# Residual loads on ScalarE's queue, the last conv rows kept on chip, and a conv layer norm in smaller steps

## The chip, the cores and the metric

The kernel runs on one core of one Trainium2 chip. The metric is the device time of one execution in microseconds; the median of three runs is the time before.

## The reference

One layer of a streaming encoder for 512 prompt frames and 64 sample frames. Only the last part matters here: a conv branch with a layer norm over channels, and one output projection over three concatenated branches, added to the scaled input and normalised.

```python
def conv_branch(a, b, left, conv_w, conv_b, ln_g, ln_b, w_pw):
    ...
    y = layer_norm(y + conv_b, ln_g, ln_b)
    y = jax.nn.silu(y) @ w_pw
    return y, up[:, -(CONV_W - 1):]

def layer_step(...):
    ca, cb, cg, q, k, v, ag, mq, mg = split_in_proj(x @ w_in)
    ...
    mix = jnp.concatenate([conv_out * jax.nn.silu(cg), att * jax.nn.silu(ag), mem * jax.nn.silu(mg)], axis=-1)
    y = layer_norm(ALPHA * x + mix @ w_out, ln_g, ln_b)
```

All is fp32, 1024 conv channels, 512 attention and 512 memory channels, model width 2048.

## The kernel before

TensorE works on pairs of reduced-precision pieces of each fp32 number: a weight block `wraw` (128 x 1024) is cast to `whi` by ScalarE (L248), and VectorE takes the rest as `wlo` (L253); a product is `hi*hi + lo*hi + hi*lo`. A *stage* is one such weight block and the matmuls that use it. `next_stage` hands out the pieces of stage i, casts the blocks up to i + 2, and loads further ones as far ahead as `AHEAD` and, for the output projection, `AHEAD_OUT` (by the block's form) say. Weight loads go out on SyncE's queue (L175); the sums of two blocks that some forms need are made by accumulating loads on GpSimd's queue (L179), of a copy that ScalarE makes (L198).

The order of the stages is fixed: V, the input projection's column pairs, keys and queries, the memory parts; then `out_pair(8, ...)` twice (14 stages each, output columns 0 to 1023 and 1024 to 2047), which multiplies the attention and memory half of the mix by its half of the output weights and stores the results in DRAM as `a_dram`; then the pointwise projection of the conv branch (8 stages, `pw`); then `out_pair(0, ...)`, the conv half for columns 0 to 1023 (14 stages, numbered 0 to 13 below); then two plain blocks of four stages for columns 1024 to 1535 and 1536 to 2047, and the last layer norm. The 14 stages of `out_pair` are seven products of two stages each, in the order of `OUT_FORMS`. TensorE's queue has stages 10 and 11 of the second call, and part of the stages behind them, right behind stage 7.

Work beside the matmuls is written as generators (`sides`), and `pump` moves each on by one `yield` after a stage. `conv_ln` is the one in `sides["norm"]`: it loads the eight channel blocks `y` of the conv from DRAM on SyncE (L964), where the conv had spilled them (L532), subtracts the mean (L971), sums squares (ScalarE squares L976, VectorE adds `s`, L977), and has TensorE sum them over the partitions (`var`, L985). Then come `rs` on VectorE, a power on GpSimd (L990), a diagonal `dg` on VectorE, `ra` and `rb` on TensorE (L999, L1000), copies to `rstd` on ScalarE (L1002), a multiply and a Silu for each block (L1005, L1006). `split_sx` makes the hi and lo pieces `sx` (L1018, L1019) that the pointwise stages use.

`z[t, n]` is the residual and the result, one tile for each of five token tiles t and four column blocks n. `load_z` loads a piece of x on SyncE (L1165), multiplies it by ALPHA on ScalarE (L1166) and adds `a_dram` by an accumulating load on GpSimd (L1167). The z of columns 0 to 1023 are loaded from the pointwise stage 3 on, one or two a stage; the other ten partly inside `out_pair(0, ...)` and partly when it has been written out. The tile scheduler keeps for each engine the order in which it takes the instructions; each engine waits in that order.

Of the kernel before, what the change touches and what calls it, by code (L numbers as in the profile page):

```python
# [51 lines left out]
AHEAD_OUT = {"a11": 5, "s1": 6, "s2": 0, "a12": 4, "s3": 6, "s4": 6, "a22": 4}  # L52
# [76 lines left out]
def hymba_kernel(ctx: ExitStack, tc: tile.TileContext, wst, xT, memT, xp, xs, kcT, vc, mkcT, mvc, biasx,  # L129
# [368 lines left out]
    def queue_conv(j):  # L498
# [24 lines left out]
        def last():  # L523
            t = TAPS - 1
            y = t6([P, NT], "y")
            o = NP_TOK + 30
            for w, o, ys in ((HP, 0, slice(0, HP)), (HS, o, slice(HP, HALF))):
                yv = y.rearrange("p (a b) -> p a b", a=2)[:, :, ys]
                uv, av = (m.rearrange("p (a b) -> p a b", a=2)
                          for m in (up[0][:, o + t:o + t + 2 * w], acc[0][:, o:o + 2 * w]))  # L530
                nc.vector.scalar_tensor_tensor(yv, uv, cw_sb[:, j, t:t + 1], av, op0=ALU.mult, op1=ALU.add)
            spill.append(lambda: nc.gpsimd.dma_start(y_dram[j], y))  # L532
            if j == 0:
                s1[0] = y
            elif j == 1:
                y0, s1[0] = s1[0], t6([P, NT], "s1")
                nc.vector.tensor_add(s1[0], y0, y)
            else:
                nc.vector.tensor_add(s1[0], s1[0], y)
            if j == NCB - 1:  # L540
                sides["norm"].append(conv_ln())
# [417 lines left out]
    def conv_ln():  # L959
        yield  # L960
        spill.pop()()
        for j in range(NCB):
# [7 lines left out]
        for j in range(NCB):  # L970
# [7 lines left out]
            if j == 3:  # L978
# [25 lines left out]
        for j in range(NCB):  # L1004
            nc.vector.tensor_mul(ysb[j], ysb[j], rstd)  # L1005
            nc.scalar.activation(ysb[j], ysb[j], AF.Silu, bias=cp_sb[:, 2, j:j + 1], scale=cp_sb[:, 1, j:j + 1])  # L1006
            if j == 3:
                yield
        for j in range(SX_EARLY):
            split_sx(j)  # L1010
        ln_left[0] = False
# [146 lines left out]

    def load_z(n, tiles=range(5)):

        for t in tiles:
            rows = P if t < 4 else NS_TOK
            ns = slice(n * 512, (n + 1) * 512)
            zt = z[t, n] = t5([P, 512], "z")
            nc.sync.dma_start(zt[:rows], xp[t * P:(t + 1) * P, ns] if t < 4 else xs[:, ns])  # L1165
            nc.scalar.mul(zt[:rows], zt[:rows], ALPHA)  # L1166
            nc.gpsimd.dma_start(zt[:rows], a_dram[t, n][:rows], accum_op=ALU.add)  # L1167
# [79 lines left out]
    for j in range(NCB):  # L1247
# [10 lines left out]
        if j >= 3:  # L1258
            load_z((j - 3) // 3, ((0, 1), (2, 3), (4,))[(j - 3) % 3])
# [69 lines left out]

    def conv_forms(stage):  # L1330
        if stage < 4:
            form234(stage, alloc_large)

# [18 lines left out]
    def zsample(i, acc):  # L1352
        zsum(4, i, out_source(4, acc))
        done(4, i)
        if i == 0:
            load_z(2, range(2))

    sub = nc.vector.tensor_sub
    load_z(1, (4,))
# [3 lines left out]
    load_z(2, range(2, 5))  # L1363
    load_z(3)
    g = load_g(2)
    accs, sacc = tileB(mlhs2, range(4), msl, list(range(8)))
# [117 lines left out]
```

## Time and profile before

| | us |
|---|---|
| median of three runs | 962.25 |
| lowest and highest | 959.97 and 962.35 |
| the profiled execution | 963.6 |
| its span | 961.8 |
| TensorE's matmuls busy | 931.7 |
| VectorE, ScalarE, GpSimd busy | 740.1, 480.4, 145.3 |
| mean granted TensorE clock | 0.981 |

The profile is of one execution. In the rows below times are from the start of the span; L and a number is a line of the kernel; `PE`, `DVE`, `ACT`, `POOL` and `SP` are TensorE, VectorE, ScalarE, GpSimd and SyncE, and a q behind a name its queue of DMA issues. Granted clock 1.00 is 2.4 GHz and .50 is 1.2 GHz. What stands in brackets is how long the engine was idle before the instruction, and what ended that.

### The profile page before, as it was taken

What the parts mean: (1) busy time and instruction counts of PE and PEld (TensorE: products, weight loads), DVE (VectorE), ACT (ScalarE), POOL (GpSimd) and SP (SyncE); (2) the same over time, 40 slices, a digit from 0 to 9 for tenths busy, and PEclk for the clock granted to TensorE, in tenths of its full rate; (3) what the DMA queues carried; (4) which work ended last, traced back from release to release, by engine and by line L of the source; (5) the groups of instructions that cost most, each with busy time, mean ns of one, the idle gap of its engine ahead of it and who ended that gap; (6) DMA issues with size and microseconds to landing.
All of it is one profiled execution on the core that took longest, in us unless ns stands there. A gap on an engine that the chain in (4) does not pass through costs nothing. (4 is left out here: it accounts for less than half of the span.)

```text
span 961.8 us, 15450 instructions
## 1 busy us (share of the span) xinstructions
PE 931.7 (97%) x5965; PEld 855.8 (89%) x5965; DVE 740.1 (77%) x1075; ACT 480.4 (50%) x805; POOL 145.3 (15%) x215
## 2 busy tenths in 40 slices
PE   8999999999999999999999999999988999978995
PEld 5899999999999999999999888998866899955873
DVE  7968986996799797688999564299998766737566
ACT  6655444454544444554554466646768643742200
POOL 0020000100110000011110001100122211333451
PEclk9999999999999999999999999999999999987997
DMA  9755566555666766589766558863883976996304
GB/s 327 208 171 147 145 164 174 160 147 165 198 178 173 195 169 184 183 233 242 181 173 167 165 175 225 211 156 80 198 268 105 248 279 183 196 217 204 98 19 179
DMA packets 61996, 175.34 MB, mean 182 GB/s; under 512 B 7710, under 2 KB 12318, under 8 KB 61922
## 3 DMA queue, kind: packets, MB, share of 16 engines
q1 hardware_dynamic: 41602, 111.92, 34.9%
q0 software_dynamic: 16720, 54.91, 28.1%
q10 hardware_dynamic: 3600, 7.52, 2.2%
q8 instruction: 47, 0.77, 0.3%
q14 instruction: 27, 0.22, 0.1%
HBM read 150.69 MB, written 23.63 MB: 181 GB/s over the span
## 5 line engine op out<-in xcount | busy, mean ns | idle before, releaser
L248 ACT CAST whi<-wraw 128x1024 fp32r<-128x1024 f32 x195 | 203.3, 1050 | 188.6 <-PE st L556 51.4
L253 DVE TENSOR_TENSOR wlo<-wraw,whi 128x1024 fp32r<-128x1024 f32 x173 | 215.2, 1247 | 95.1 <-ACT whi L248 48.0
L556 PE MATMUL st<-x,whi 128*128 128x288 f32 x1024 | 204.6, 295 | 0.0
L519 DVE SCALAR_TENSOR_TENSOR acc<-up,cw_sb,acc 128x606 f32<-128x606 f32 x232 | 196.5, 847 | 4.1
L556 PEld LDWEIGHTS st<-x,whi 128*128 128x128 f32 x1024 | 164.1, 188 | 0.3 <-ACT neg L625 0.2
L556 PE MATMUL st<-x,wlo 128*128 128x288 f32 x512 | 151.1, 295 | 0.0
L315 PE MATMUL accA<-x,whi 128*128 128x288 f32 x768 | 134.9, 298 | 0.0
L315 PEld LDWEIGHTS accA<-x,whi 128*128 128x128 f32 x768 | 112.8, 189 | 1.6 <-issue 0.8
L556 PEld LDWEIGHTS st<-x,wlo 128*128 128x128 f32 x512 | 96.1, 188 | 0.0
L315 PE MATMUL accA<-x,wlo 128*128 128x288 f32 x384 | 82.3, 296 | 0.0
L556 PE MATMUL st<-t13h,wlo 128*128 128x288 f32 x256 | 75.6, 295 | 0.0
L556 PE MATMUL st<-t13l,whi 128*128 128x288 f32 x256 | 75.5, 295 | 0.0
L556 PE MATMUL st<-t13h,whi 128*128 128x288 f32 x256 | 75.5, 295 | 0.0
L1116 PE MATMUL ob<-whi,mix 128*128 128x512 f32 x176 | 58.6, 413 | 4.5 <-ACT whi L248 4.5
L315 PEld LDWEIGHTS accA<-x,wlo 128*128 128x128 f32 x384 | 61.8, 189 | 0.0
L179 POOL DMA_DIRECT2D wraw<-in_wst_dram x27 | 27.1, 1003 | 177.5 <-DVE pos L612 60.1
L556 PE MATMUL st<-t,whi 128*128 128x288 f32 x256 | 51.3, 295 | 0.0
L179 POOL DMA_DIRECT2D wsum<-in_wst_dram x22 | 21.4, 974 | 190.1 <-ACT wsum L209 115.9
L556 PEld LDWEIGHTS st<-t13h,whi 128*128 128x128 f32 x256 | 48.1, 188 | 0.0
L556 PEld LDWEIGHTS st<-t13l,whi 128*128 128x128 f32 x256 | 48.1, 188 | 0.0
L556 PEld LDWEIGHTS st<-t13h,wlo 128*128 128x128 f32 x256 | 48.1, 188 | 0.0
L235 DVE TENSOR_TENSOR wraw<-wraw,wraw 128x1024 f32<-128x1024 f32 x33 | 40.2, 1218 | 7.5 <-DMA wraw<-in_wst_dram 7.3
(390 smaller groups left out, 1859.6 us busy)
## 6 DMA issues: line engine op xcount, KB each, us to landing
wraw<-in_wst_dram SPq DMA_DIRECT2D x151, 512.0 KB, 4.3
wraw<-in_wst_dram POOLq DMA_DIRECT2D x27, 512.0 KB, 8.1
wsum<-in_wst_dram POOLq DMA_DIRECT2D x22, 512.0 KB, 7.7
wlo<-in_wst_dram POOLq DMA_DIRECT2D x22, 512.0 KB, 7.3
xraw<-in_xT_dram SPq DMA_DIRECT2D x19, 288.0 KB, 6.3
ad<-c POOLq DMA_DIRECT2D x16, 256.0 KB, 4.7
z<-in_xp_dram SPq DMA_DIRECT2D x16, 256.0 KB, 10.1
z<-ad POOLq DMA_DIRECT2D x16, 256.0 KB, 7.0
```

The costliest lines, as they stand in the source:

```text
L179: nc.gpsimd.dma_start(dst, wst[where[b]], accum_op=ALU.add)
L235: nc.vector.tensor_add(a21, a21, w_fetch(q[{"s1": "a22", "s2": "a11", "s4": "a12"}[form]]))
L248: nc.scalar.copy(hi, src)
L253: nc.vector.tensor_sub(lo, src, hi.bitcast(F32))
L315: nc.tensor.matmul(acc[:, :HALF], stat[:, ws], mv[:, c], start=ki == 0 and pi == 0, stop=ki == len(klist) - 1 and pi == 2)
L519: nc.vector.scalar_tensor_tensor(acc[0], up[0][:, t:t + ACCW], cw_sb[:, j, t:t + 1], acc[0], op0=ALU.mult, op1=ALU.add)
L556: nc.tensor.matmul(acc[:, :HALF], stat[:, ws], mv, start=first and k == 0 and i == 0, stop=k == 7 and i == 2, skip_group_check=not first)
L1116: nc.tensor.matmul(a, stat[:, os_], mv[:, ws], start=first and ki == 0 and i == 0, stop=ki == 3 and i == 2, skip_group_check=not first)
```

## The change

Four things are done.

- `AHEAD_OUT` rises by one for three forms, so their blocks are loaded a stage earlier.
- The last block of conv rows, `y` 7, is written into a `t5` buffer and stays there; it is neither spilled nor loaded.
- `conv_ln` begins five steps after it is queued, not one, loads seven blocks, and yields after every second block in the loops (subtraction, Silu, `sx`), where it yielded once in the first two and not in the third.
- `load_z` loads on ScalarE's queue and only notes the tile; `form_z` multiplies and accumulates later. Columns 0 to 1023 are loaded in the pointwise stages 0 to 5; the ten z of the others one a stage from stage 8 of `out_pair(0, ...)` as written, and two a stage in the block behind it.

```diff
@@ -49,7 +49,7 @@
 AHEAD_PAIRS = 7
 SX_EARLY = 5
 OUT_FORMS = ("a11", "s1", "s2", "a12", "s3", "s4", "a22")
-AHEAD_OUT = {"a11": 5, "s1": 6, "s2": 0, "a12": 4, "s3": 6, "s4": 6, "a22": 4}
+AHEAD_OUT = {"a11": 5, "s1": 6, "s2": 0, "a12": 5, "s3": 7, "s4": 6, "a22": 5}
 
 
 def quads(pair):
@@ -522,14 +522,17 @@
 
         def last():
             t = TAPS - 1
-            y = t6([P, NT], "y")
+            y = t6([P, NT], "y") if j < NCB - 1 else t5([P, NT], "y")
             o = NP_TOK + 30
             for w, o, ys in ((HP, 0, slice(0, HP)), (HS, o, slice(HP, HALF))):
                 yv = y.rearrange("p (a b) -> p a b", a=2)[:, :, ys]
                 uv, av = (m.rearrange("p (a b) -> p a b", a=2)
                           for m in (up[0][:, o + t:o + t + 2 * w], acc[0][:, o:o + 2 * w]))
                 nc.vector.scalar_tensor_tensor(yv, uv, cw_sb[:, j, t:t + 1], av, op0=ALU.mult, op1=ALU.add)
-            spill.append(lambda: nc.gpsimd.dma_start(y_dram[j], y))
+            if j < NCB - 1:
+                spill.append(lambda: nc.gpsimd.dma_start(y_dram[j], y))
+            else:
+                ysb[j] = y
             if j == 0:
                 s1[0] = y
             elif j == 1:
@@ -957,9 +960,9 @@
         return a, b
 
     def conv_ln():
-        yield
-        spill.pop()()
-        for j in range(NCB):
+        for _ in range(5):
+            yield
+        for j in range(NCB - 1):
             ysb[j] = t5([P, NT], "y")
             nc.sync.dma_start(ysb[j], y_dram[j])
         a, b = bcast_sum(s1[0], "mean")
@@ -975,7 +978,7 @@
                 sq = t6([P, NT], "sq")
                 nc.scalar.activation(sq, ysb[j], AF.Square)
                 nc.vector.tensor_add(s2, s2, sq)
-            if j == 3:
+            if j % 2:
                 yield
         yield
         yield
@@ -1004,10 +1007,12 @@
         for j in range(NCB):
             nc.vector.tensor_mul(ysb[j], ysb[j], rstd)
             nc.scalar.activation(ysb[j], ysb[j], AF.Silu, bias=cp_sb[:, 2, j:j + 1], scale=cp_sb[:, 1, j:j + 1])
-            if j == 3:
+            if j % 2:
                 yield
         for j in range(SX_EARLY):
             split_sx(j)
+            if j % 2:
+                yield
         ln_left[0] = False
 
     shi, slo = [], []
@@ -1156,15 +1161,24 @@
 
     z = {}
 
+    zload = deque()
+
     def load_z(n, tiles=range(5)):
 
         for t in tiles:
             rows = P if t < 4 else NS_TOK
             ns = slice(n * 512, (n + 1) * 512)
-            zt = z[t, n] = t5([P, 512], "z")
-            nc.sync.dma_start(zt[:rows], xp[t * P:(t + 1) * P, ns] if t < 4 else xs[:, ns])
-            nc.scalar.mul(zt[:rows], zt[:rows], ALPHA)
-            nc.gpsimd.dma_start(zt[:rows], a_dram[t, n][:rows], accum_op=ALU.add)
+            z[t, n] = t5([P, 512], "z")
+            nc.scalar.dma_start(z[t, n][:rows], xp[t * P:(t + 1) * P, ns] if t < 4 else xs[:, ns])
+            zload.append((t, n))
+
+    def form_z(count):
+
+        for _ in range(min(count, len(zload))):
+            t, n = zload.popleft()
+            zt = z[t, n][:P if t < 4 else NS_TOK]
+            nc.scalar.mul(zt, zt, ALPHA)
+            nc.gpsimd.dma_start(zt, a_dram[t, n][:P if t < 4 else NS_TOK], accum_op=ALU.add)
 
     a_dram = {(t, n): dram([P, 512], "ad") for t in range(5) for n in range(4)}
 
@@ -1255,8 +1269,9 @@
         split_mix(j)
         if j in (1, 2, 3, 4):
             form1(j - 1, True)
-        if j >= 3:
-            load_z((j - 3) // 3, ((0, 1), (2, 3), (4,))[(j - 3) % 3])
+        form_z(2)
+        if j < 6:
+            load_z(j // 3, ((0, 1), (2, 3), (4,))[j % 3])
     drain()
 
 
@@ -1327,9 +1342,19 @@
         return spool.tile([P, 4, P] if i == 3 else [P, 2, HP], F32R, tag="t5" if i == 2 else "t9",
                           bufs=N5 if i == 2 else KD, name=nm(name))
 
+    ztiles = [(t, n) for n in (2, 3) for t in range(5)]
+
+    def next_z(count):
+        form_z(count)
+        for _ in range(min(count, len(ztiles))):
+            t, n = ztiles.pop(0)
+            load_z(n, (t,))
+
     def conv_forms(stage):
         if stage < 4:
             form234(stage, alloc_large)
+        elif stage >= 8:
+            next_z(1)
 
     def zsum(t, n, acc, op=None):
         zt = z[t, n][:P if t < 4 else NS_TOK]
@@ -1352,18 +1377,16 @@
     def zsample(i, acc):
         zsum(4, i, out_source(4, acc))
         done(4, i)
-        if i == 0:
-            load_z(2, range(2))
 
     sub = nc.vector.tensor_sub
-    load_z(1, (4,))
+    form_z(2)
     out_pair(0, {"p1": zsink(0, 0, False), "p5": zsink(1, 1, False, sub), "p16": zsink(1, 0, False),
                  "p2": zsink(0, 0, True), "p167": zsink(1, 1, True, sub), "p53": zsink(1, 0, True),
                  "p1674": zsink(0, 1, True, sub), "sample": zsample}, conv_forms)
-    load_z(2, range(2, 5))
-    load_z(3)
     g = load_g(2)
-    accs, sacc = tileB(mlhs2, range(4), msl, list(range(8)))
+    accs, sacc = tileB(mlhs2, range(4), msl, list(range(8)), before=lambda s: next_z(2))
+    while zload:
+        next_z(2)
     gs = (g, load_g(3))
     for t in range(4):
         settle(t, 2, accs[t], g, False)
```

What this does to the engines' order is shown at three places. Lines of the changed kernel are some numbers further down: the z load is its L1172, the multiply L1180, the accumulate L1181.

ScalarE, in `out_pair(0, ...)`, before: `z` with L1166 is the multiply, `whi` the casts of stages 7 to 11, `ztmp` the copy of a sample result.

```order
L1166 ACTIVATE z_9177<-z_9177 128x512
L1166 ACTIVATE z_9181<-z_9181 128x512
L248 CAST whi_9104<-wraw_9064 128x1024
L1166 ACTIVATE z_9327<-z_9327 128x512
L248 CAST whi_9125<-wsum_9027 128x1024
L1166 ACTIVATE z_9331<-z_9331 128x512
L1166 ACTIVATE z_9335<-z_9335 64x512
L248 CAST whi_9145<-wsum_9066 128x1024
L1166 ACTIVATE z_9339<-z_9339 128x512
L248 CAST whi_9185<-wraw_8751 128x1024
L1166 ACTIVATE z_9343<-z_9343 128x512
L248 CAST whi_9203<-wraw_8823 128x1024
```

And in the changed kernel, where `whi_9062` is the cast of stage 5 and `whi_9122` that of stage 8:

```order
L1172 DMA z_9176<-in_xp_dram 128x512
L198 COPY wsum_9029<-wraw_8764 128x1024
L248 CAST whi_9062<-wraw_8832 128x1024
L1180 ACTIVATE z_9176<-z_9176 128x512
L1172 DMA z_9198<-in_xp_dram 128x512
L248 CAST whi_9084<-wraw_8983 128x1024
L1172 DMA z_9226<-in_xp_dram 128x512
L1180 ACTIVATE z_9198<-z_9198 128x512
L1172 DMA z_9248<-in_xp_dram 128x512
L248 CAST whi_9101<-wraw_9027 128x1024
L1180 ACTIVATE z_9226<-z_9226 128x512
L248 CAST whi_9122<-wsum_8985 128x1024
```

The loads of z stand on ScalarE's own queue among the casts, each multiply one to four rows behind its load. It goes on in that way: the multiply of `z_9248`, the cast of stage 9, two loads, the cast of stage 10, a multiply, a load, two multiplies, the cast of stage 11.

SyncE, same place, before: the weights of stages 6 (`wraw_9025`) and 7 (`wraw_9064`), with seven z loads around them, and then those of stages 12 and on.

```order
L175 DMA wraw_9025<-in_wst_dram 128x1024
L1165 DMA z_9177<-in_xp_dram 128x512
L1165 DMA z_9181<-in_xp_dram 128x512
L175 DMA wraw_9064<-in_wst_dram 128x1024
L1165 DMA z_9327<-in_xp_dram 128x512
L1165 DMA z_9331<-in_xp_dram 128x512
L1165 DMA z_9335<-in_xs_dram 64x512
L1165 DMA z_9339<-in_xp_dram 128x512
L1165 DMA z_9343<-in_xp_dram 128x512
L175 DMA wraw_9189<-in_wst_dram 128x1024
L175 DMA wraw_9207<-in_wst_dram 128x1024
L175 DMA wraw_9209<-in_wst_dram 128x1024
```

In the changed kernel, where `wraw_8983` and `wraw_9027` are the weights of stages 6 and 7 and `wraw_9146` those of stage 12:

```order
L175 DMA wraw_8766<-in_wst_dram 128x1024
L1284 DMA gbraw_8918<-in_lngb_dram 5x512
L175 DMA wraw_8832<-in_wst_dram 128x1024
L175 DMA wraw_8983<-in_wst_dram 128x1024
L175 DMA wraw_9027<-in_wst_dram 128x1024
L175 DMA wraw_9146<-in_wst_dram 128x1024
L175 DMA wraw_9182<-in_wst_dram 128x1024
L175 DMA wraw_9204<-in_wst_dram 128x1024
```

No z load stands between the weights any more.

TensorE, at the seam of the two `out_pair(8, ...)`, before: `var` is the sum of squares, `ob` and `os` with `t_1094` and `xd` the end of the first pair, `mix_7302` the start of the second.

```order
L1116 MATMUL ob_1024_7332<-wlo_7833,t_1094_7628 128x512
L1120 MATMUL os_1061_7482<-whi_7832,xd_7432 128x512
L1122 MATMUL os_1061_7482<-wlo_7833,xd_7432 128x512
L985 MATMUL var_7911<-ones,s_1130_7817 128x1 x4
L985 MATMUL var_7911<-ones,s_1130_7817 64x1
L1116 MATMUL ob_1151_7938<-whi_7871,mix_7302 128x512 x2
L1116 MATMUL ob_1152_7939<-whi_7871,mix_7302 128x512 x2
L1120 MATMUL os_1153_7940<-whi_7871,mixsamp_7305 128x512
```

In the changed kernel, in the second pair, from the end of stage 7 (`mixsamp_7424`, `wlo_8040`) into stage 8 (`whi_8061`):

```order
L988 MATMUL var_8081<-ones,s_1144_7910 128x1 x4
L988 MATMUL var_8081<-ones,s_1144_7910 64x1
L1127 MATMUL os_1131_7868<-wlo_8040,mixsamp_7424 128x512
L1121 MATMUL ob_1129_7866<-whi_8061,t23h_7428 128x512
L1121 MATMUL ob_1129_7866<-whi_8061,t23l_7429 128x512
L1121 MATMUL ob_1129_7866<-wlo_8062,t23h_7428 128x512
L1121 MATMUL ob_1130_7867<-whi_8061,t23h_7428 128x512
L1121 MATMUL ob_1130_7867<-whi_8061,t23l_7429 128x512
L1121 MATMUL ob_1130_7867<-wlo_8062,t23h_7428 128x512
L1121 MATMUL ob_1129_7866<-whi_8061,t23h_7494 128x512
L1121 MATMUL ob_1129_7866<-whi_8061,t23l_7495 128x512
L1121 MATMUL ob_1129_7866<-wlo_8062,t23h_7494 128x512
```

`var` has moved from the seam to the end of the second pair's stage 7; `ra`, which stood in that pair's stage 1, is the next row behind these, after nine matmuls of stage 8.

## Rows read from the trace of the kernel before

**Rows 1.** page, busy us (share of the span) and instructions of each engine.

```profile
PE 931.7 (97%) x5965; PEld 855.8 (89%) x5965; DVE 740.1 (77%) x1075; ACT 480.4 (50%) x805; POOL 145.3 (15%) x215
```

**Rows 2.** windows: stretch, its length, busy us of each engine, PE clock, DMA share, GB/s.

```profile
777.00:797.00 20.00, 20.00 (x152) 20.00 (x151) 12.42 (x20) 9.19 (x15) 1.62 (x3) 1.00 0.63 214
695.00:750.00 55.00, 49.57 (x207) 39.01 (x206) 46.64 (x67) 36.93 (x52) 14.16 (x18) 0.94 0.63 188
850.00:895.00 45.00, 35.52 (x118) 25.33 (x117) 30.77 (x34) 18.00 (x22) 19.92 (x16) 0.81 0.78 207
```

**Rows 3.** windows of 5 us in the first of the two stretches.

```profile
725.00:730.00 5.00, 5.00 (x22) 4.08 (x20) 3.42 (x8) 1.07 (x3) 3.70 (x3) 0.72 0.20 74
745.00:750.00 5.00, 5.00 (x16) 3.92 (x16) 3.50 (x3) 3.64 (x5) 3.14 (x4) 0.67 0.80 139
```

**Rows 4.** waits of PE, 690 to 750: us in total, times, longest.

```profile
PE var L985 <- DVE s L977: 2.6, 1, 2.6
PE ob L1116 <- ACT whi L248: 1.7, 1, 1.7
```

**Rows 5.** timeline of ACT, 684 to 746: start, us, instruction, count, idle before.

```profile
731.99 6.19 ACT L1006 ACTIVATE y<-y,cp_sb 128x576 f32<-128x576 f32 x8
738.09 2.96 ACT L1018 CAST sx<-y 128x576 fp32r<-128x576 f32 x5
```

**Rows 6.** timeline of PE, 846 to 894.

```profile
845.65 0.39 PE L1116 MATMUL ob<-whi,t23h 128*128 128x512 f32 x1
...
850.19 0.39 PE L1122 MATMUL os<-wlo,mixsamp 128*128 128x512 f32 x1
854.92 1.22 PE L1116 MATMUL ob<-whi,mix 128*128 128x512 f32 x2 [4.34 <-ACT whi L248]
...
876.67 0.63 PE L343 MATMUL accB<-whi,mix 128*128 128x512 f32 x1
...
893.81 0.40 PE L343 MATMUL accB<-whi,mix 128*128 128x512 f32 x1
```

**Rows 7.** timeline of ACT, 836 to 878.

```profile
843.91 0.63 ACT L1166 ACTIVATE z<-z 128x512 f32<-128x512 f32 x1 [1.92 <-DVE z L1336]
849.96 0.63 ACT L1166 ACTIVATE z<-z 128x512 f32<-128x512 f32 x1 [5.42 <-DMA z<-in_xp_dram]
853.82 1.04 ACT L248 CAST whi<-wraw 128x1024 fp32r<-128x1024 f32 x1 [3.23 <-DMA wraw<-in_wst_dram]
...
869.84 1.04 ACT L248 CAST whi<-wraw 128x1024 fp32r<-128x1024 f32 x1 [5.92 <-DMA wraw<-in_wst_dram]
```

**Rows 8.** timeline of SP's queue, 780 to 895.

```profile
809.09 1.26 SPq L1165 DMA_DIRECT2D z<-in_xp_dram  x2
...
838.80 1.71 SPq L1165 DMA_DIRECT2D z<-in_xp_dram  x2
840.62 0.38 SPq L175 DMA_DIRECT2D wraw<-in_wst_dram  x1
...
863.26 5.76 SPq L175 DMA_DIRECT2D wraw<-in_wst_dram  x5
877.63 0.33 SPq L1165 DMA_DIRECT2D z<-in_xp_dram  x1
```

**Rows 9.** timeline of all engines, 724 to 729.5.

```profile
725.02 2.59 POOL L990 TENSOR_TENSOR rs<-rs,mhalf 128x8 f32<-128x8 f32 x1 [1.63 <-DVE rs L989]
...
728.84 0.83 PE L999 MATMUL ra<-dg,ones 128*128 128x128 f32 x6
```

**Rows 10.** DMA issues of ACT's queue: count, KB each, median us to landing.

```profile
gated<-neg ACTq DMA_DIRECT2D x8, 288.0 KB, 4.4
```

**Rows 11.** timeline of ACT, 800 to 882.

```profile
817.35 0.63 ACT L1166 ACTIVATE z<-z 128x512 f32<-128x512 f32 x1 [4.79 <-DMA z<-in_xp_dram]
...
880.68 0.63 ACT L1166 ACTIVATE z<-z 128x512 f32<-128x512 f32 x1 [3.19 <-DMA z<-in_xp_dram]
```

**Rows 12.** page, DMA issues: count, KB each, median us to landing.

```profile
z<-in_xp_dram SPq DMA_DIRECT2D x16, 256.0 KB, 10.1
```

## The prediction

> **What bounds the kernel now.** I read the busy shares first: TensorE's matmuls fill 97% of the span [rows 1], so only TensorE's own losses matter, and there are two kinds, idle time and a slow clock. The windows show where they are. A good stretch, 777 to 797, has PE busy for all of its 20 us at granted clock 1.00; two stretches have not [rows 2].
>
> *Stretch A*, 695 to 750, the conv layer norm: busy 49.57 of 55, so 5.4 us idle [rows 2]. Two of its 5-us windows ran slow: 5.00 us at .72 and 5.00 at .67 [rows 3], so 1.40 + 1.65 = 3.1 us lost. **A costs 8.5 us.** The reader is to see the causes on PE's waits: 2.6 us until DVE's sum of squares is there for `var`, 1.7 us until ScalarE casts a weight [rows 4]. That cast was late because eight Silu (6.19 us) and five `sx` casts (2.96 us) stood ahead of it on ScalarE in one block [rows 5].
>
> *Stretch B*, 850 to 895, the first half of the last output projection: busy 35.52 of 45, so 9.5 us idle, at mean clock .81 [rows 2], another 0.19 x 35.5 = 6.7 us. **B costs 16.2 us.** Its longest wait, 4.34 us, names ScalarE's weight cast as what ended it [rows 6], so the question goes to ScalarE's queue: it waited 5.42 us for a z load, 3.23 and 5.92 us for weight loads [rows 7]. SyncE's queue says why the weights were late: z loads went out between them from 838.80, and the next weight could not go out until 863.26 [rows 8].
>
> **The change part by part.** *Last conv rows on chip.* One store and one load fewer, both off TensorE's path: nothing by itself.
>
> *Layer norm in smaller steps.* `var` and its inputs move from the seam between the two output pairs to the end of the second pair's stage 7, and all weight casts of that pair stand ahead of the Silu block. So the 2.6 us wait, the 1.7 us wait with the half us behind it, and their slow clocks go, and the seven loads no longer go out in one row: up to 8.5 us. What is late next is `ra`. It stands ten matmuls behind `var` there, and its chain is DVE's `rs`, a few tenths, then GpSimd's power at 725.02 (2.59 us), DVE's `dg`, and PE's `ra` at 728.84 [rows 9]: 3.8 us from the power on, 4.1 in all. At full clock twenty matmuls run from 845.65 to 850.19 [rows 6], 0.227 each, so ten cover 2.3 us. With some 0.3 us for `var` itself to end PE waits 2.1 us. The idle of 2.6 us ahead of `var` was followed by the 1.4 us of slow clock [rows 3, 4]; I charge that again. A's gain is 8.5 - 2.1 - 1.4 = **5.0 us**. Lower end: `rs`, the power and `dg` can each stand behind one other instruction of about 1.2 us, such as a weight split or an accumulate issue; then the wait is 5.5 us, the clock costs 1.65, and 1.3 us is left. The upper end is 8.5, with other work of PE's in the gap. The rest of the chain, the table load, the Silu and `sx` blocks [rows 5] with three more casts and the last copies, takes about 18 us, against 16 us of matmuls behind `ra`; the first pointwise stage eats `sx` one block after another and needs the last some 5 us after its start, so some 3 to 4 us of cover are left. If that is gone, each us late costs one.
>
> *Weights earlier.* Without z loads on SyncE, stage 7's weights go out ahead of all of this (now 840.62 [rows 8]), and stage 12's wait only for stage 8's split, not stage 10's. The 4.34 us wait loses this cause.
>
> *z through ScalarE's queue.* The first ten z are loaded three steps earlier in the pointwise stages, where PE is fully busy [rows 2] and the next use is far: nothing, either way. For the last ten the order on ScalarE is the matter: load, two weight items, multiply, load, cast, load, multiply, and so on. The multiply waits for its transfer on ScalarE itself, the weight casts of stages 6 to 11 are queued behind it, and TensorE waits for those. Up to the cast of stage 11 five landings stand in series. An issue takes 0.33 us on SyncE when nothing holds it [rows 8], and I take it to overlap ScalarE's work; the multiply takes 0.63 us, a cast 1.04 [rows 7]. The first load goes out behind the last `t` cast, where ScalarE is now at about 838.9. With L for a landing the cast of stage 11 then ends at 838.9 + 5L + 5 x 0.6 (the multiplies between) + 2 x 1.0 (the casts that no landing covers, the last among them) = 843.9 + 5L.
>
> L is not in the trace for this queue; the nearest rows are these. The z load of 838.80, same place, same size, no weight directly ahead of it: its multiply began at 843.91, so 5.1 us [rows 7, 8]. Lower end 3.05 us: 877.63 to 880.68 [rows 8, 11]. Upper end 8.3 us: 809.09 to 817.35, right behind a weight in its queue [rows 8, 11]. ScalarE's own queue landed 288 KB stores in 4.4 us in the middle [rows 10], but elsewhere and outward. I take **5.1**, the row from the same place. The median of all z loads on SyncE's queue is 10.1 [rows 12]; there they shared a queue with 512 KB weights, which they no longer do, so I leave it out as an end.
>
> With 5.1: stage 7's cast ends at 851.4 (PE is through with stage 6 at about 850.4, so 1.0 idle); stage 10's, next on PE, at 858.1 (PE through at 855.1, 3 idle, then half clock, twelve at twice 0.227 = 5.4); stage 11's at 869.4 (about 6 idle, again half clock). Stage 11 and the eight sample matmuls behind it end at about 876.7, as now [rows 6]. Only then does it gain: the 60 matmuls from there to 893.8 take 17.1 us now [rows 6], since the clock is still low behind the waits before them (as behind those in [rows 3]) and some wait; at full clock, with the casts of stages 12 to 14 done early, 60 x 0.227 = 13.6. **B's gain is 3.5 us.** Each us of L moves it by five: 9 at L = 4.0, 13.5 at 3.1 (where little of PE's own waits is left to lose), nothing at 5.8, minus 12.5 at 8.3.
>
> *A rule weighed against it.* The row: DMA's share in the second stretch is .78 on average with 207 GB/s [rows 2], so transfers there already crowd each other.
> The Trainium skill, "DMA: Bandwidth & Descriptors", section "Issuing engines are not separate DMA queues", says that DMAs issued by different engines end up on the same 16 DMA engines and interleave there, and that a second issuer saves only the time of the issue. By it alone the move buys nothing in L, and the third rival below would be the forecast.
> The same page's "Queues, rings and completion order" has each DMA engine go round robin between the queues, which lets a z load pass the weights that are queued ahead on SyncE's; it speaks for an L below the 8.3 of the row behind a weight.
>
> **The sum.** 5.0 + 3.5 = 8.5 us. The profiled execution took 963.6 us, 1.35 above the median of the runs; 963.6 - 8.5 = 955.1 by itself, and against the median 962.25 - 8.5 = **953.8 us**. Within this case L may lie between 3.6 and 5.8 and A's gain between 4 and 6: 946 to 958.
>
> **Rivals.** *One: the loads land like the fastest rows.* L near 3.05, since a z load has its queue for itself. Stage 11's cast ends at 859.2, stage 10 never waits, B gains 13.5; with A's 5.0, 943.8 us. For it: 3.05 us at 877.63. Against: that was a quieter stretch.
>
> *Two: nothing is left.* The layer norm swaps its wait for a longer one at `ra` (A gains 1.3), and L is at its balance point of 5.8 (B gains 0): 961.0. For it: `rs`, power and `dg` are on three queues that are all in use; against: DVE and GpSimd have idle time there.
>
> *Three, slower: ScalarE is held by each landing.* Five landings in series with weight casts behind each, at 8.3 us: B loses 12.5, A gains 5.0, 969.8 us. It decides from L = 5.8 + 5.0 / 5 = 6.8, and shows as slower from 7.4. For it: 8.3 us at 809.09 in a stretch with less traffic, and ScalarE's own 5.42 us wait for a z in this place [rows 7]. Against: the 5.1 us and the stores' 4.4.
> This is the rival for which the Trainium skill's rule on issuing engines speaks.
>
> **How the numbers follow.** Forecast 0.54, rival one 0.17, two 0.14, three 0.15. A measurement of this kernel tells 0.3%, 2.9 us, from no change: below 959.4 is faster, above 965.1 slower. Faster 0.54 + 0.17 = 0.71; same 0.14; slower 0.15. The range 942 to 966 takes in the forecast, rival two, nearly all of rival one and the mild end of rival three; about 0.17 is left out.
>
> **What would show it.** Right for A: `var` without a wait in the second pair, `ra` with a wait of about 2 us, no wait for a cast behind the Silu block, the pointwise stages beginning about 5 us earlier. Right for B: ScalarE idle five times until a z landed, about 4 us or more each, PE idle twice, before stages 10 and 11, and at full clock from the last sample matmul on. Wrong: z landings of 3 us (rival one) or 8 (rival three); a wait at the first pointwise stage; weight loads that still go out late on SyncE for another reason; the scattered y loads delaying weights of the second pair.

## The result, and the profile of the changed kernel

The changed kernel took a median of 952.07 us (948.75 to 954.38, four runs), the kernel before 962.17 beside it: ratio 0.9898, interval 0.9860 to 0.9935. That is 10.1 us less; 953.8 us was forecast. The profiled execution took 953.8 us, 1.7 above its median, with a span of 952.0.

Three seams tell where the time went. On TensorE the pointwise stages begin at 768.00 (before: 776.54, read from the same view), the last projection's first half at 819.18 (before: 827.73), and the first `accB` row behind that half at 883.86 (before: 893.81, [rows 6]). The timeline of PE (start, us, instruction, count), first two lines of the kernel before, then four of the changed kernel; the row at 865.18 is the first behind the sample matmuls:

```profile
776.54 0.69 PE L315 MATMUL accA<-sx,whi 128*128 128x288 f32 x4
...
827.73 0.63 PE L1116 MATMUL ob<-whi,mix 128*128 128x512 f32 x2
```
```profile
768.00 0.69 PE L315 MATMUL accA<-sx,whi 128*128 128x288 f32 x4
...
819.18 0.63 PE L1121 MATMUL ob<-whi,mix 128*128 128x512 f32 x2
...
865.18 0.50 PE L343 MATMUL accB<-whi,mix 128*128 128x512 f32 x1
...
883.86 0.40 PE L343 MATMUL accB<-whi,mix 128*128 128x512 f32 x1
```

So the layer norm's stretch gained 8.5 us, the pointwise stages nothing, and the last projection's first half, 66.1 us before and 64.7 now, 1.4 us. Inside that half PE was at the row behind the sample matmuls after 48.9 us before (876.67, [rows 6]) and after 46.0 now; it gained 2.9 us up to there and lost 1.5 again behind it. The windows answer to [rows 2, 3] (stretch, its length, then busy us of PE, PEld, DVE, ACT and POOL, PE clock, DMA share, GB/s):

```profile
695.00:750.00 55.00, 54.38 (x242) 44.05 (x240) 44.65 (x57) 32.00 (x43) 14.62 (x19) 1.00 0.89 257
750.00:755.00 5.00, 4.84 (x25) 4.09 (x26) 3.41 (x9) 2.57 (x5) 0.00 (x0) 1.00 0.32 101
845.00:895.00 50.00, 40.50 (x145) 29.81 (x145) 38.73 (x37) 16.78 (x20) 20.84 (x19) 0.86 0.62 172
875.00:880.00 5.00, 4.22 (x12) 3.03 (x11) 5.00 (x7) 0.00 (x0) 2.35 (x2) 0.66 0.63 211
```

In the first stretch PE is busy for 54.4 of 55 us, where it was 49.57, and its clock stays at 1.00. In the window from 845 the old picture is still there: 9.5 us idle in 50 us, mean clock .86. The waits of PE between 690 and 900 name who ended them (in total, times, longest), to be held against [rows 4, 6]:

```profile
PE ob L1121 <- ACT whi L248: 4.4, 2, 2.7
PE ob L1121 <- DVE wlo L253: 2.8, 2, 2.2
PE accB L345 <- DVE wlo L253: 1.5, 1, 1.5
PE ob L1121 <- DVE z L1361: 0.8, 1, 0.8
PE ra L1002 <- DVE dg L997: 0.8, 1, 0.8
```

`var` and the cast behind the Silu block no longer stand there; `ra` is the new wait, 0.8 us. In the last projection the one long wait for a cast (4.34 us, [rows 6]) has become two, 1.7 and 2.7 us, and the waits for VectorE's splits (`wlo`), of at most 1.0 us before, have grown to 2.2 and 1.5. No cast waited for a weight load in this half any more; before, two did, 3.2 and 5.9 us [rows 7].

ScalarE's timeline there, with its queue's issues (ACTq), answers to [rows 7]:

```profile
828.55 0.33 ACTq L1172 DMA_DIRECT2D z<-in_xp_dram  x1
...
833.43 0.63 ACT L1180 ACTIVATE z<-z 128x512 f32<-128x512 f32 x1 [2.49 <-DMA z<-in_xp_dram]
833.43 0.89 ACTq L1172 DMA_DIRECT2D z<-in_xp_dram  x2
...
837.86 0.63 ACT L1180 ACTIVATE z<-z 128x512 f32<-128x512 f32 x1 [2.86 <-DMA z<-in_xp_dram]
837.87 0.33 ACTq L1172 DMA_DIRECT2D z<-in_xp_dram  x1
...
843.40 0.63 ACT L1180 ACTIVATE z<-z 128x512 f32<-128x512 f32 x1 [2.50 <-DMA z<-in_xp_dram]
843.49 0.47 ACTq L1172 DMA_DIRECT2D z<-in_xs_dram  x1
...
846.27 1.04 ACT L248 CAST whi<-wraw 128x1024 fp32r<-128x1024 f32 x1 [1.29 <-DVE wlo L253]
...
849.29 0.63 ACT L1180 ACTIVATE z<-z 64x512 f32<-64x512 f32 x1 [1.97 <-DMA z<-in_xs_dram]
849.29 0.33 ACTq L1172 DMA_DIRECT2D z<-in_xp_dram  x1
...
853.84 0.63 ACT L1180 ACTIVATE z<-z 128x512 f32<-128x512 f32 x1 [1.02 <-DMA z<-in_xp_dram]
854.37 1.03 ACT L248 CAST whi<-wraw 128x1024 fp32r<-128x1024 f32 x1
```

This is the predicted series: load 828.55, multiply 833.43; 833.43 and 837.86; 837.87 and 843.40; 843.49 and 849.29; 849.29 and 853.84. Five landings, 4.9, 4.4, 5.5, 5.8 and 4.6 us, 5.0 on average; each load but the first was issued only when the multiply ahead of it began. Behind the last stands the cast of stage 11, and PE waited 2.7 us for it. The cast of stage 10 is the one at 846.27; it waited for a split, which followed the cast of stage 9 behind the third landing.

### The profile page after: what moved, and what is told of

The parts are those of the page before. It is cut to its first block, busy times and chain, and to the rows that moved or that the text cites. A ratio compares the mean times of both kernels' runs of the same rounds, so it can differ in the third digit from the quotient of the medians.

```text
span 952.0 us, 15428 instructions
## 1 busy us (share of the span) xinstructions
PE 926.2 (97%) x5965; PEld 853.1 (90%) x5965; DVE 743.7 (78%) x1075; ACT 479.2 (50%) x805; POOL 142.1 (15%) x214
## 5 line engine op out<-in xcount | busy, mean ns | idle before, releaser
L253 DVE TENSOR_TENSOR wlo<-wraw,whi 128x1024 fp32r<-128x1024 f32 x173 | 219.0, 1269 | 78.3 <-ACT whi L248 40.0
```

Source lines behind the costliest of these rows:

```text
L253: nc.vector.tensor_sub(lo, src, hi.bitcast(F32))
```

## The experiments

Of each kernel the median, its ratio to the kernel before on the same chip with the interval, and, from its profiled execution, two seams: the start of the pointwise stages (776.5 before, 768.0 changed) and the length of the last projection's first half up to its last `ob` matmul (65.6 and 64.2). These lengths come from one execution each, and executions of the changed kernel lie up to 5.6 us apart, so a difference of 2 us between two such lengths is not evidence by itself.

### Each part alone: the layer norm, and z

The layer norm's steps, the rows on chip and the weights' lead, with z as before:

```diff
-            nc.scalar.dma_start(z[t, n][:rows], ...)
-            zload.append((t, n))
+            nc.sync.dma_start(zt[:rows], ...)
+            nc.scalar.mul(zt[:rows], zt[:rows], ALPHA)
+            nc.gpsimd.dma_start(zt[:rows], a_dram[t, n][:rows], accum_op=ALU.add)
...
-        form_z(2)
-        if j < 6:
-            load_z(j // 3, ((0, 1), (2, 3), (4,))[j % 3])
+        if j >= 3:
+            load_z((j - 3) // 3, ((0, 1), (2, 3), (4,))[(j - 3) % 3])
```

> The z loads are put back as they were before (on SyncE's queue, at the old places); the layer norm in small steps, the last conv rows on chip and the earlier weights stay. Theory one, from the seams of the two traces: the layer norm stretch alone gained 8.5 us (the pointwise stages begin at 768.0 instead of 776.5) and the z loads 1.4, so this kernel gains about 8.5 and takes 953 to 954 us. Theory two, the terms as predicted: the layer norm gives 5.0 us and z 3.5, so it takes about 957. In its trace the first theory wants the pointwise stages to begin at about 768 and the 4 us wait ahead of stage 7 in the last projection to be back.

Measured: 951.82 us, 0.9909 (0.9889 to 0.9930); pointwise stages at 767.7. The waits of PE in its last projection:

```profile
PE ob L1121 <- ACT whi L248: 8.8, 1, 8.8
```

The old wait is back, 8.8 us long and ahead of stage 10 now, not of stage 7: with the loads on SyncE's queue at the old places, too, the casts of stages 7 to 9 stand behind multiplies that wait for a z. And yet the kernel is as fast as the full change: PE waited 10.7 us in that half in all, against 9.5 in the changed kernel, where the waits are shorter and more.

The kernel before with z alone moved (the same diff the other way round):

> The kernel before with one part alone: z loaded on ScalarE's queue and formed later, at the changed kernel's places; layer norm, conv rows and the weights' lead as before. Theory one: it gains what the seams give for the last projection, 1.4 us, so about 960.8. Theory two, the terms as predicted: 3.5 us, about 958.7. A third outcome: below 957, the z loads also help the layer norm's stretch, or their gain is hidden in the full kernel by something that the layer norm leaves behind.

Measured: 959.81 us, 0.9972 (0.9956 to 0.9987); pointwise stages at 777.6, the projection's half 62.0 us long.

The layer norm alone carries the whole gain: 10.4 us without z's move against 10.1 with it, each against its own runs of the kernel before. z's move alone gains 2.4 us, and on top of the layer norm nothing that these runs can tell. The 3.6 us by which it shortens the projection's half alone are near the 3.5 of the prediction, but they don't add.

### The weights' lead

```diff
-AHEAD_OUT = {"a11": 5, "s1": 6, "s2": 0, "a12": 5, "s3": 7, "s4": 6, "a22": 5}
+AHEAD_OUT = {"a11": 5, "s1": 6, "s2": 0, "a12": 4, "s3": 6, "s4": 6, "a22": 4}
```

> The changed kernel with the old lead of the output projection's weights (4, 6, 4 stages instead of 5, 7, 5). Theory one: the lead decides nothing, since SyncE's queue waits for free weight buffers anyway: 951 to 953, as the changed kernel. Theory two: the earlier weights carry the last projection's gain and part of the layer norm's: 954 to 957.

Measured: 952.28 us, 0.9904 (0.9884 to 0.9924). The lead decides nothing here.

### The queue: one word changed

```diff
-            nc.scalar.dma_start(z[t, n][:rows], ...)
+            nc.sync.dma_start(z[t, n][:rows], ...)
```

> The changed kernel with one word changed: the z loads go out on SyncE's queue, written at the same places. Theory one, the queue matters because SyncE's queue is taken in order: seven z loads stand in a row between the weights of stages 7 and 12, land one behind the other, and push those weights back: 2 to 5 us slower than the changed kernel, 954 to 957. Theory two, from the Trainium skill, 'DMA: Bandwidth & Descriptors', section 'Issuing engines are not separate DMA queues': the issuer saves only the time of the issue, so it takes the same as the changed kernel, about 952. A third outcome, faster than 950: on SyncE the loads go out earlier than ScalarE lets them, and ScalarE's multiplies no longer wait.

Measured: 944.92 us, 0.9825 (0.9803 to 0.9847): the third outcome, 7.2 us faster than the changed kernel. SyncE's queue and ScalarE in its trace:

```profile
825.88 3.44 SPq L1172 DMA_DIRECT2D z<-in_xp_dram  x4
...
831.24 2.14 SPq L1172 DMA_DIRECT2D z<-in_xp_dram  x2
```

```profile
833.36 0.63 ACT L1180 ACTIVATE z<-z 128x512 f32<-128x512 f32 x1 [5.31 <-DMA z<-in_xp_dram]
...
839.04 1.03 ACT L248 CAST whi<-wraw 128x1024 fp32r<-128x1024 f32 x1
```

The seven loads (the fifth, not shown, at 829.75) go out from 825.88 on without a multiply between them, and several are under way at once. ScalarE waits 5.3 us for the first and 0.9, 1.1 and 0.4 for the next three, where on its own queue each next load could only go out when the multiply ahead of it had been reached. The cast of stage 11 ends 29.4 us after the projection's start, 36.2 in the changed kernel, and PE waits 0.7 us for casts there instead of 4.4.

By the Trainium skill ("DMA: Bandwidth & Descriptors", section "Issuing engines are not separate DMA queues") a second issuer saves only the time of the issue. Here the choice of the issuer was worth 7.2 us, because an issue takes its turn among the engine's own instructions; what a queue does to the bandwidth, these runs do not separate.

The edit moves all twenty z loads, the ten of the pointwise stages too. There, in the changed kernel, ScalarE also waits for landings:

```profile
810.77 0.63 ACT L1180 ACTIVATE z<-z 128x512 f32<-128x512 f32 x1 [3.31 <-DMA z<-in_xp_dram]
...
816.16 0.63 ACT L1180 ACTIVATE z<-z 64x512 f32<-64x512 f32 x1 [3.08 <-DMA z<-in_xs_dram]
```

It comes to the last projection's first `t23h` cast at 823.29, with the loads on SyncE's queue at 820.51. So a part of the 7.2 us belongs to this place.

### Is it the queue or the row of landings

```diff
     def next_z(count):
-        form_z(count)
+        form_z(min(count, max(0, len(zload) - 2)))
...
-    while zload:
-        next_z(2)
+    form_z(len(zload))
```

> The changed kernel, z still on ScalarE's queue, but each multiply is written two calls behind its load, so that two or three loads are under way at a time. Theory one: what cost the last projection its gain is the row of landings that stand one behind the other on ScalarE (load, multiply, load, multiply), not the queue as such. Then most of the 7 us that the loads on SyncE's queue gained come back here too: stage 11's cast ends some 5 us earlier, and the kernel takes 946 to 949 us. Theory two: a DMA that ScalarE issues lands later or holds ScalarE, whatever stands between load and multiply; then it stays at 951 to 953.

Measured: 945.66 us, 0.9828 (0.9810 to 0.9845). Still on ScalarE's queue, with two or three loads under way at a time, it is within a microsecond of the kernel with SyncE's queue. So most of the cost was the row of landings, and not the queue as such. Its profiled execution, with 949.4 us the slowest of the four, shows only a part of this. From the first late load to the end of stage 11's cast it is 23.3 us, 26.9 in the changed kernel. But the first late load goes out 13.9 us after the projection's start, not 9.4, after ScalarE had waited 6.6 us for a z of the pointwise stages, so in that execution the cast comes no earlier.

### GpSimd beside VectorE's splits

The second loss in the projection stands on VectorE. Its splits in the changed kernel, and GpSimd at the same time (timelines of DVE and of POOL):

```profile
847.35 1.23 DVE L253 TENSOR_TENSOR wlo<-wraw,whi 128x1024 fp32r<-128x1024 f32 x1 [1.11 <-ACT whi L248]
...
856.53 2.75 DVE L253 TENSOR_TENSOR wlo<-wraw,whi 128x1024 fp32r<-128x1024 f32 x1
...
870.23 5.54 DVE L253 TENSOR_TENSOR wlo<-wraw,whi 128x1024 fp32r<-128x1024 f32 x2
```

```profile
855.32 2.86 POOL L1367 TENSOR_TENSOR z<-z,gb 128x512 f32<-128x512 f32 x2
...
870.67 2.87 POOL L1367 TENSOR_TENSOR z<-z,gb 128x512 f32<-128x512 f32 x2
```

A split takes 1.23 us; the one at 856.53, beside GpSimd's multiplications of z from 855.32 to 858.18, took 2.75, and the two from 870.23, beside those from 870.67, 5.54 (4.41 of it the first). PE waited 2.2 and 1.5 us for them, and its clock fell behind the waits (.66 in the window from 875 above).

Leaving those ten multiplications out:

```diff
-        nc.gpsimd.tensor_mul(zt, zt, gpair[n][:rows])
```

> The changed kernel without GpSimd's ten multiplications of z by the layer norm's gain for columns 0 to 1023 (they are left out). Theory one: VectorE's weight splits waited for them, one took 2.75 us instead of 1.23 beside a GpSimd multiply and a pair took 5.54, and TensorE then waited 2.2 and 1.5 us for a split: without them those two waits and the slow clock behind them go, 3 to 5 us, so 947 to 949 us. Theory two: the splits are late because ScalarE's casts are, and GpSimd costs nothing on the path: 951 to 953, with the waits ended by a cast in the split's place.

Measured: 946.97 us, 0.9847 (0.9822 to 0.9873), 5.1 us less than the changed kernel. The same two splits in its trace:

```profile
859.65 1.21 DVE L253 TENSOR_TENSOR wlo<-wraw,whi 128x1024 fp32r<-128x1024 f32 x1
...
872.50 2.41 DVE L253 TENSOR_TENSOR wlo<-wraw,whi 128x1024 fp32r<-128x1024 f32 x2
```

1.21 us for one and 2.41 for two. The gain itself does not show in this execution, which took 950.4 us, the most of the four: PE waits at most 1.0 us for a split, but longer for casts.

```profile
PE ob L1121 <- ACT whi L248: 6.1, 4, 3.6
```

The runs, 945.46 to 950.39 us, also overlap a little with those of the changed kernel, 948.75 to 954.38. So this experiment alone is weak, and the next two have to bear it out. Moving the multiplications behind the last accumulate of z instead (`formed` is that accumulate):

```diff
...
-        nc.gpsimd.tensor_mul(zt, zt, gpair[n][:rows])
+        gbmul.append((t, n))
...
+    with tc.issue_after(formed[0].ins):
+        for t, n in gbmul:
+            zt = z[t, n][:P if t < 4 else NS_TOK]
+            nc.gpsimd.tensor_mul(zt, zt, gpair[n][:P if t < 4 else NS_TOK])
     gs = (g, load_g(3))
```

> The changed kernel with one thing moved: GpSimd's ten multiplications behind the last accumulate of z. Theory one: it gains what leaving them out gained, 5 us, so 946 to 948. Theory two: it gains less, since the multiplications now fall beside the splits of the last block: 949 to 952.

Measured: 947.47 us, 0.9843 (0.9814 to 0.9872). It gains as much as leaving them out, within what the runs can tell (946.64 to 951.55). With z on SyncE's queue as well:

> z on SyncE's queue at the changed kernel's places, which took 944.9, and GpSimd's ten multiplications put behind the last accumulate of z, where TensorE has the next weights already. Theory one (GpSimd's reads hold VectorE's splits): the waits for splits at 854, 857 and 868 of that kernel's trace shrink, 2 to 4 us less: 941 to 943. Theory two: nothing to win there, 944 to 946. If the multiplications are in the way later, it gets slower than 946.

Measured: 939.16 us, 0.9770 (0.9745 to 0.9796). The two gains, 7.2 and 4.6 us, add up to 11.8; 12.9 were measured. The traces of the two kernels on SyncE's queue show it at the right place: with the multiplications in the projection PE waits 4.3 us for splits between 690 and 900, with the multiplications late 1.0, and the projection's half is 58.5 and 53.6 us long.

The multiplications now stand in a row beside two splits of the next block (timelines of POOL and DVE):

```profile
877.65 12.77 POOL L1395 TENSOR_TENSOR z<-z,gb 128x512 f32<-128x512 f32 x10
```
```profile
877.77 15.06 DVE L253 TENSOR_TENSOR wlo<-wraw,whi 128x1024 fp32r<-128x1024 f32 x2 [1.44 <-ACT whi L248]
```

The first of these two splits took 13.75 us, until 1.1 us behind the last of the ten multiplications. PE did not wait for it: it had the next weights already.

The Trainium skill, "SBUF — State Buffer", section "Who interferes with whom", says that a VectorE instruction with two SBUF inputs contends with a GpSimd instruction that reads SBUF, and that the ports they share are an exclusive lock. The traces agree that they contend: the split reads two tiles, and 856.53 to 859.28 is the rest of GpSimd's pair, to 858.18, and 1.1 us behind it. The section speaks of one instruction against another; here the split waited for all of GpSimd's row, for two and for ten. At 870.23 it did so although, by the profile, it had begun 0.44 us ahead of the pair (4.41 us, to 1.1 us behind the pair's end at 873.54).

### The multiplies behind the casts, on either queue

To the last kernel one thing more is done: each multiply of a late z is queued on ScalarE behind the last weight cast that is written ahead of it.

```diff
-            nc.scalar.copy(hi, src)
+            lastcast[0] = nc.scalar.copy(hi, src)
...
     def next_z(count):
-        form_z(count)
+        with tc.issue_after(lastcast[0].ins):
+            form_z(count)
```

> z loaded on SyncE's queue, GpSimd's ten multiplications late (as in the kernel of 939.2), and each multiply of a late z queued on ScalarE behind the last weight cast written ahead of it, so that the casts of stages 6 to 10 wait for no landing. Theory one: what is left in the last projection, 2.7 us ahead of stage 10 with its slow clock, is the last of ScalarE's waits for z; without it 936 to 938. Theory two: the casts then wait for their weights or for free buffers instead, and it stays at 939.

Measured: 936.86 us, 0.9724 (0.9701 to 0.9746). The projection's half is 49.1 us long, and PE's waits from 690 to 900 and its window are

```profile
PE ra L1003 <- DVE dg L998: 0.8, 1, 0.8
PE os L1128 <- DVE wlo L254: 0.6, 1, 0.6
```

```profile
845.00:890.00 45.00, 44.30 (x191) 35.42 (x190) 39.05 (x34) 15.08 (x20) 21.19 (x21) 1.00 0.65 173
```

with the clock at 1.00 throughout. This is the fastest kernel of the study, 15 us below the changed one.

> The same kernel with the loads on ScalarE's queue, as in the changed kernel. Theory one: the queue itself costs nothing, only the landings that stand in front of casts did; then this takes the same as the one on SyncE's queue, within 1.5 us of it. Theory two: an issue on ScalarE's queue holds ScalarE, or its loads land later; then it is 2 us or more behind that one.

Measured: 939.51 us, 0.9753 (0.9730 to 0.9777), its runs from 939.04 to 940.68 against 936.71 to 936.91: 2.65 us behind, the number of theory two. The first late load goes out at 832.42 on ScalarE's queue and at 825.92 on SyncE's, while the projection starts at 818.9 and 818.8. ScalarE's timeline on its own queue says why:

```profile
815.37 0.63 ACT L1181 ACTIVATE z<-z 128x512 f32<-128x512 f32 x1 [7.14 <-DMA z<-in_xp_dram]
...
832.42 0.34 ACTq L1173 DMA_DIRECT2D z<-in_xp_dram  x1
```

The edit moves only the multiplies of the late ten. Those of the pointwise stages still wait for their landings, the last two of these for 7.1 us and (at 820.02) 2.3, ahead of the projection's first casts; with the loads on SyncE's queue ScalarE waits at most 1.0 us for a z between 790 and 820, and comes to the first `t23h` cast at 820.57 instead of 827.15. So there were still landings ahead of casts, and the 2.65 us do not show that the queue as such costs anything. A kernel with those multiplies behind the casts as well was not run, so this stays open.

### Start and step size of the layer norm

The changed kernel with coarse steps and the late start:

```diff
-            if j % 2:
+            if j == 3:
                 yield
...
             split_sx(j)
-            if j % 2:
-                yield
```

> The changed kernel with the layer norm's steps as coarse as before (one yield in the middle of each loop), but still begun five steps late and with the last rows on chip. Theory one: what gained 8.5 us is the later start, which puts the sum of squares and the Silu block into the middle of the second pair, behind casts that are done; then the coarse kernel takes the same, 951 to 953. Theory two: the small steps matter, since a block of eight Silu and five casts again keeps a weight cast waiting: 954 to 957, with a wait for a cast in the second pair.

Measured: 954.87 us, 0.9937 (0.9911 to 0.9963); pointwise stages at 770.9. ScalarE, and PE behind it:

```profile
748.35 6.19 ACT L1009 ACTIVATE y<-y,cp_sb 128x576 f32<-128x576 f32 x8
754.45 2.95 ACT L1021 CAST sx<-y 128x576 fp32r<-128x576 f32 x5
```

```profile
758.07 0.50 PE L1119 MATMUL ob<-whi,t23h 128*128 128x512 f32 x1 [1.59 <-ACT c L1198]
```

Eight Silu and five `sx` casts stand in one block again, the copies of a result bank (`c`, at 757.42) wait behind them, and PE waits 1.6 us for that bank. It had also waited 1.0 us at `var`. And the changed kernel with small steps and the old start:

```diff
-        for _ in range(5):
+        for _ in range(1):
             yield
```

> The changed kernel with the layer norm's small steps, but begun one step after it is queued, as before, not five. With coarse steps and the late start the pointwise stages began at 770.9, with both at 768.0, with neither at 776.5. Theory one: start and step size each do a part and add up; then the early start costs about 5.7 us, the pointwise stages begin at 773 to 774 and the kernel takes 956 to 958 us. Theory two: either alone does most of it, since each moves the sum of squares away from the seam of the two pairs; then they begin at 769 to 771 and it takes 952 to 955.

Measured: 950.58 us, 0.9874 (0.9841 to 0.9907); pointwise stages at 766.2, and its window

```profile
695.00:760.00 65.00, 65.00 (x294) 53.36 (x293) 57.89 (x81) 47.80 (x65) 16.89 (x23) 1.00 0.82 242
```

shows no loss at all: PE busy for 65.00 of 65 us at clock 1.00. Neither theory said that. With coarse steps the late start brought 5.7 us (776.5 to 770.9), but the small steps with the old start do the whole work of this stretch; on top of them the late start adds nothing and brings the 0.8 us wait at `ra`. All these kernels keep the last conv rows on chip, which was not undone alone. The trace of the kernel before speaks against a part of the rows in the gain: between 670 and 730 VectorE, which reads `y`, never waited for a load.

## Why the prediction was right, point by point

**The time.** 953.8 was forecast, 952.07 came; the total is right, but two of its terms were off in opposite ways: 5.0 us for the layer norm where 8.5 came, and 3.5 for the projection where the profiled execution shows 1.4. That sum came out well partly by luck. By the runs it is more luck still: without z's move the kernel takes 951.82 us, so the layer norm's steps, with the rows and the lead, bring all of the gain, and z's move, in the changed kernel, nothing that shows.

**The layer norm.** Which waits go was right: `var` and the cast behind the Silu block are gone, with their slow clocks. That `ra` would be the next wait was right, and its size was not: 2.1 us and 1.4 of slow clock were charged, 0.8 us and no slow clock came. The step that failed is the chain's length, 4.1 us, read from the power at 725.02 to `ra` at 728.84 [rows 9]. That `ra` row has no wait in front of it: there PE came to `ra` only when the matmuls ahead were done, so the row gave the order's time and not the chain's. The rows of the changed kernel, where PE does wait, give it (timelines of DVE, POOL and PE):

```profile
746.89 0.16 DVE L991 TENSOR_SCALAR rs<-var 128x4 f32<-128x4 f32 x1 [0.67 <-PE var L988]
...
749.81 1.03 DVE L997 TENSOR_SCALAR dg<-ident,rs 128x128 f32<-128x128 f32 x5 [1.58 <-POOL rs L993]
```
```profile
747.19 2.59 POOL L993 TENSOR_TENSOR rs<-rs,mhalf 128x8 f32<-128x8 f32 x1
```
```profile
745.59 1.26 PE L988 MATMUL var<-ones,s 128*128 128x1 f32 x10
746.78 0.50 PE L1127 MATMUL os<-wlo,mixsamp 128*128 128x512 f32 x1
...
750.16 1.16 PE L1002 MATMUL ra<-dg,ones 128*128 128x128 f32 x8 [0.77 <-DVE dg L997]
```

From `rs` at 746.89 to `ra` at 750.16 it is 3.3 us: `ra` began while the five pieces of `dg` were still being made, to 750.84. The ten matmuls from 746.78 cover 2.6. The rest of the charge, the clock, went with it: the window from 750, behind the wait, shows 1.00. The price of the whole stretch, 8.5 us, was too small too: the kernel with small steps and the old start, in which nothing is lost there, begins the pointwise stages 10.3 us earlier than the kernel before. The cover of the Silu and `sx` blocks held, as worked out: no wait at the first pointwise stage.

**z on ScalarE's queue.** The series of landings was right, the place of the gain was not. There were five landings in series, stages 7 to 11 cast behind them, PE waiting ahead of stages 10 and 11 (1.7 and 2.7 us; 3 and 6 forecast, and none ahead of stage 7, where 1.0 was). The landing was right: 5.1 forecast, 5.0 measured. ScalarE's idle times were not about 4 us each, as the signs had it, but 1.0 to 2.9, since casts and a copy fill a part of each landing. The cast of stage 11 ended 36.2 us after the projection's start, 41.7 were forecast. Some 2 us of that are an earlier first load; most of the rest is that an issue does not wait for the multiply ahead of it to end (833.43 in both rows above), which I had charged each time, and that a landing covered one more cast.

So PE came to the row behind the sample matmuls 2.9 us earlier, where I had forecast no gain, and it would have been more without the 2.2 us wait for stage 11's split. The step that failed is the next one, the one from which all of the 3.5 us were to come: the 60 matmuls behind the sample matmuls at full clock, 13.6 us against 17.1 before. They took 18.7, from 865.18 to 883.86. Casts were on time there; the splits were not, held by GpSimd, and the clock fell behind PE's waits. Nothing of GpSimd's ten multiplications was in the prediction. The trace of the kernel before has the same thing: two splits in 4.53 us, beside two of the multiplications from 882.35. PE did not wait for them there.

```profile
882.77 4.53 DVE L253 TENSOR_TENSOR wlo<-wraw,whi 128x1024 fp32r<-128x1024 f32 x2
```

For the first ten z, those of the pointwise stages, I had charged nothing, either way. That was wrong for ScalarE: it waited 3.3 and 3.1 us for their landings, and its first casts for the projection came later for it. What this cost by itself was not measured; where nothing else of z stood ahead of casts, the two queues lay 2.65 us apart.

**Weights earlier, rows on chip.** Nothing was charged for the first beyond the cause that it takes from the 4.34 us wait, and undoing the lead alone changed nothing. Without z loads between them the weights were there in time, as forecast. The rows on chip were not tried alone.

**The rivals.** One and three hung on a landing of 3.05 and 8.3 us; neither came. Two, a longer wait at `ra`, did not come. The third rival's mechanism, ScalarE held by landings, is what happened with shorter landings: against the same loads on SyncE's queue it cost 7.2 us. The forecast compared it with the old kernel's waits alone and so called it a gain.

## What to carry to other kernels

A DMA on a compute engine's queue goes out when that engine reaches it, and a consumer of the data on the same engine, one or two instructions later, makes every landing a stop for all that stands behind: put the loads on the queue of an engine that does no such work, and the consumer behind the work that others wait for. Split a long block of small work into steps that fit between the instructions the critical engine waits for; where it began mattered here only while the steps were coarse. When a chain's length is read from a trace, read it from a row that shows a wait, else it is the order's time.

## What the runs showed of the hardware

- A VectorE split of 128 x 1024 with two SBUF inputs took 1.23 us by itself, 2.75 and 4.41 beside a pair of GpSimd multiplications that read SBUF, and 13.75 beside a row of ten; each time it ended 1.1 us behind the last of them. Moving the ten multiplications gained 4.6 us, and 5.8 with z on SyncE's queue.
- An issue on ScalarE's queue overlaps the instruction ahead of it: 833.43 is the start of both the multiply and the next load's issue.
- An idle of 0.8 us in full work left the granted clock at 1.00 (window from 750), while behind the waits at 847 to 860, 1.7, 0.5, 2.7 and 2.2 us, the mean over 845 to 895 was .86.
